# The second top-16 of a product-key router: 112 candidate sums instead of 256, and index lookups four heads at a time

## The chip, the cores and the metric

The kernel runs on one core of a Trainium2 chip. The metric is the device time of one execution in microseconds. The engines are named as in the profile: PE (TensorE matmul), PEld (its weight load), DVE (VectorE), ACT (ScalarE), POOL (GpSimd) and SP (SyncE, which issues most DMAs).

## The reference, cut to what matters

Two layers of a transformer over 256 latent and 256 context tokens. Each layer mixes tokens (attention, Fourier mixing, pooling) and then runs a feed-forward layer of 16,384 single-neuron experts, from which every token picks with product keys:

```
q = (h @ w_pq).reshape(B, L, 8, 2, 128)
s = einsum("blhpd,hpkd->blhpk", q, peer_keys)            # 8 heads, 2 halves, 128 keys
sv, si = top_k(s, 16)
cand = (sv[..., 0, :, None] + sv[..., 1, None, :]).reshape(B, L, 8, 256)
cidx = (si[..., 0, :, None] * 128 + si[..., 1, None, :]).reshape(B, L, 8, 256)
top_s, pos = top_k(cand, 16)
eidx = take_along_axis(cidx, pos, axis=-1)
gate = softmax(top_s, axis=-1)
```

So per token and head, 16 of 256 pair sums are selected, and the place of each selected sum says which first-half key and which second-half key it belongs to. Then `a = gelu(down[eidx] . h)`, and the output is the sum of `gate * a * up[eidx]`. Layer 0 does this for context and latent tokens, layer 1 for the latent ones only.

## The kernel before, in words

Tokens lie in blocks of 128, one token per partition. `scores` makes the key scores of two blocks and selects the best 16 of 128 of every half (`sv`, `si`). `topk` (L556) then does the second selection for one block on DVE: for each of 8 heads it adds the 16 x 16 pair sums (L562) and calls `top16` (L547 to L554), which finds eight maxima (L549), their places (L550), removes them (L551), and finds eight more (L553, L554). Behind the heads it copies the index table to bf16 (L568), makes the softmax gate (L571 to L575), splits the place `pos` into its two digits (L577, L578, L580), and looks the two key numbers up: for each half `w` and each two heads, a one-hot table of 32 x 16 is made by comparison with `iota16` (L586), multiplied by the index table (L589) and summed over its 16 columns (L591). `topk` is a generator; it yields twice a head and once a lookup, 24 times in all.

It is called six times. `early_routes` runs it twice, as the filler `extra` inside `front(0, 1, ...)`, the attention stage of the latent half of layer 0: `front` takes one step of the filler at six points of each of its 8 heads and drains the rest before the last projection. From the second of these calls come the expert numbers (L652) with which POOL then gathers rows of the expert tables (`rows`, L669). `routes` runs it twice in layer 0 and twice in layer 1: first a call alone, woven with `early` units (`fill`), then `gates` of the first block interleaved with a second call, woven with more units, and at last `gates` of the second block. How many units go with each step is fixed by the rates `R0` and `R1`.

A unit of `early` is `down` (L701 on): a 512 KB load of expert weights by SP in two parts, a split of each into a high and a low part on ACT (L83) and DVE (L84), 24 matmuls on PE (L93 to L95, 384 columns in layer 0, 256 in layer 1), a Gelu on ACT (L707) and a store. `gates` (L617 on) makes, for every four tokens, a comparison on DVE (L628, 1024 bf16 columns), a product (L632) and 12 matmuls of 128 columns (L638), and stores the expert gates; for a block of 128 tokens that is 32 times.

Working tiles come from tagged pools: `f1` (6 slots), `f2` (15 slots of 2 KB a partition) and `f8`. A tile that finds no free slot makes its first writer wait until a slot is released; a load waits on SP's queue, which runs in order.

Of the kernel before, what the change touches and what calls it, by code (L numbers as in the profile page):

```python
# [12 lines left out]
BF = mybir.dt.bfloat16  # L13
U32 = mybir.dt.uint32
I32 = mybir.dt.int32
AF = mybir.ActivationFunctionType
OP = mybir.AluOpType
AX = mybir.AxisListType
# [4 lines left out]
NH = 8  # L23
# [18 lines left out]
class Net:  # L42
# [101 lines left out]
    def setup2(self):  # L144
        nc, c, h = self.nc, self.c, self.h

        def ld(name, shape):
            t = c.tile(shape, F32, name=name)
            nc.sync.dma_start(t, h[name])
            return t  # L150

        self.g2 = ld("g2", [128, 2, 8])
        self.qg = ld("qg", [128, 2, 2])
        self.kg = ld("kg", [128, 2])
        self.bg = ld("bg", [128, 2, 24])
        self.hbg = c.tile([128, 2, 24], F32, name="hbg")
        nc.vector.tensor_scalar(self.hbg, self.bg, 0.5, None, op0=OP.mult)
        self.pscale = ld("pscale", [128, 2, 2])
        self.dup = ld("dup", [128, 128])
        self.tab = ld("tab", [128, TT])  # L160
        nc.sync.dma_start(self.xT[:, :, T:TT], h["xt"][:, :, T:TT])
        it = self.f1([128, 128])
        nc.sync.dma_start(it, h["iota"])
        self.iota = c.tile([128, 64, 2], BF, name="iotab")
        nc.vector.tensor_copy(self.iota.rearrange("p a b -> p (a b)"), it)
        self.iota16 = c.tile([128, 16], BF, name="iota16b")
        nc.vector.tensor_copy(self.iota16, it[:, 0:16])

    def mod_steps(self, l, *parts):
        nc, late = self.nc, None  # L170
# [385 lines left out]
    def topk(self, sv, si, out):  # L556
        nc, kp = self.nc, self.k
        ts = kp.tile([128, 8, 16], F32, name="tsc", bufs=1)
        pos = kp.tile([128, 128], U32, name="pos", bufs=1)
        for hd in range(NH):  # L560
            cd = self.f1([128, 16, 16])
            nc.vector.tensor_tensor(cd, sv[:, 2 * hd, :].unsqueeze(2).to_broadcast([128, 16, 16]),  # L562
                                    sv[:, 2 * hd + 1, :].unsqueeze(1).to_broadcast([128, 16, 16]), op=OP.add)
            scr = self.f1([128, 256])
            yield from self.top16(ts[:, hd, :], pos[:, hd * 16:(hd + 1) * 16], cd.rearrange("p a b -> p (a b)"), scr)
            yield
        sb = kp.tile([128, 16, 16], BF, name="sb", bufs=1)
        nc.vector.tensor_copy(sb, si)  # L568
        g = kp.tile([128, 8, 16], F32, name="gate", bufs=1)
        sm = kp.tile([128, 8, 2], F32, name="gsum", bufs=1)  # L570
        nc.vector.tensor_sub(g, ts, ts[:, :, 0:1].to_broadcast([128, 8, 16]))  # L571
        nc.scalar.activation(g, g, AF.Exp)
        nc.vector.reduce_sum(sm[:, :, 0], g, axis=AX.X)
        nc.vector.reciprocal(sm[:, :, 1], sm[:, :, 0])
        nc.vector.tensor_mul(g, g, sm[:, :, 1:2].to_broadcast([128, 8, 16]))  # L575
        pu = kp.tile([128, 2, 128], U32, name="pu", bufs=1)
        nc.vector.tensor_scalar(pu[:, 0, :], pos, 4, None, op0=OP.logical_shift_right)  # L577
        nc.vector.tensor_scalar(pu[:, 1, :], pos, 15, None, op0=OP.bitwise_and)  # L578
        pb = kp.tile([128, 2, 128], BF, name="pb", bufs=1)
        nc.vector.tensor_copy(pb, pu)  # L580
        ij = kp.tile([128, 2, 128], F32, name="ij", bufs=1)
        for w in range(2):
            for h2 in range(4):
                ks = slice(32 * h2, 32 * h2 + 32)
                oh = self.f1([128, 32, 16], BF)
                nc.vector.tensor_tensor(oh, self.iota16.unsqueeze(1).to_broadcast([128, 32, 16]),  # L586
                                        pb[:, w, ks].unsqueeze(2).to_broadcast([128, 32, 16]), op=OP.is_equal)
                o4 = oh.rearrange("p (h k) a -> p h k a", h=2)
                nc.vector.tensor_tensor(o4, o4, sb[:, 4 * h2 + w:4 * h2 + 4:2, :].unsqueeze(2).to_broadcast(  # L589
                    [128, 2, 16, 16]), op=OP.mult)  # L590
                nc.vector.reduce_sum(ij[:, w, ks], oh, axis=AX.X)  # L591
                yield
        out += [ij, g]

# [508 lines left out]
```

## Time and profile before

| what | value |
|---|---|
| median of three runs | 3143.14 us (3133.66 to 3145.1) |
| the profiled execution | 3146.14 us |
| its span in the profile | 3144.4 us |
| PE busy, share of the span | 2945.8 us, 94% |
| DVE busy | 2534.3 us, 81% |
| ACT busy | 1460.3 us, 46% |
| POOL busy | 323.9 us, 10% |

Busy time of an engine is time in which it ran an instruction; matmuls are pipelined and their ends are modelled, so PE shown as busy isn't PE at its peak. The profiled execution's time and its span differ by 1.7 us, which lie around the span.

### The profile page before, as it was taken

The page shows a single profiled execution, that of the slowest core. Times are in us where ns is not written, and L with a number is a line of the kernel's source. Part 1 is how long each engine was busy: PE and PEld are TensorE (multiplying, and loading weights), DVE is VectorE, ACT ScalarE, POOL GpSimd, SP SyncE. Part 2 cuts the span into 40 slices and gives each one's busy share as a digit, 9 for nine tenths or more (in the row PEclk, how much of TensorE's full clock was granted, in tenths as well). Part 3 has the DMA queues.
Part 4 walks back from the last instruction along what each step waited for, and adds up shares of the span by engine and source line. Part 5 has one row for each costly group of instructions (what it writes and reads, how often), then busy time and mean ns, then how long its engine had stood idle before and what let it go on. Part 6 is the DMA issues. An engine that isn't in the chain of part 4 may idle for free.

```text
span 3144.4 us, 55017 instructions
## 1 busy us (share of the span) xinstructions
PE 2945.8 (94%) x19215; PEld 2726.3 (87%) x19215; DVE 2534.3 (81%) x5831; ACT 1460.3 (46%) x2814; POOL 323.9 (10%) x260
## 2 busy tenths in 40 slices
PE   7999899798898999999999999999988889999998
PEld 5799878798888889999999998789877877799997
DVE  6677889798997889899999998566799966666666
ACT  5565444443444443344334434445544544555554
POOL 0000000111000121433333341000000000000000
PEclk8999999899999999999999999999998999999999
DMA  7574443675568878898988986454546788776664
GB/s 233 179 230 142 145 126 111 203 242 194 179 185 251 303 250 273 303 307 305 304 303 304 320 291 214 143 160 142 185 143 186 218 264 278 242 231 205 208 201 141
DMA packets 400719, 695.36 MB, mean 221 GB/s; under 512 B 36793, under 2 KB 148153, under 8 KB 396345
## 3 DMA queue, kind: packets, MB, share of 16 engines
q1 hardware_dynamic: 363576, 557.61, 54.8%
q0 software_dynamic: 36864, 134.23, 12.8%
q8 instruction: 151, 2.47, 0.3%
q14 instruction: 128, 1.04, 0.1%
HBM read 631.94 MB, written 59.77 MB: 220 GB/s over the span
## 4 chain that ended last, share of the span: by engine, by line
PE 65%; DVE 17%; DMA 11%; issue 5%; ACT 2%; SPq 0%; POOL 0%; DVEq 0%; ACTq 0%
PE mm L93 9%; PE mm L94 8%; PE mm L95 8%; PE acc L94 7%; PE acc L95 7%; PE acc L93 7%; DVE wl L84 4%; DMA ge<-E 2%; PE acc L818 2%; PE acc L819 2%; PE acc L817 2%; DVE a L632 2%; DMA raw<-in_up 2%; DMA raw<-in_wmod 1%; DVE f L628 1%
## 5 line engine op out<-in xcount | busy, mean ns | idle before, releaser
L83 ACT CAST wh<-raw 128x512 fp32r<-128x512 f32 x1604 | 981.4, 619 | 1006.4 <-PE acc L95 267.4
L84 DVE TENSOR_TENSOR wl<-raw,wh 128x512 fp32r<-128x512 f32 x1604 | 1075.7, 685 | 276.4 <-ACT wh L83 264.4
L93 PE MATMUL mm<-hH,wh 128*128 128x256 f32 (+1 forms) x2432 | 760.0, 313 | 43.1 <-ACT ge L707 38.9
L94 PE MATMUL mm<-hH,wl 128*128 128x256 f32 (+1 forms) x2432 | 757.1, 311 | 19.8 <-DVE wl L84 18.8
L95 PE MATMUL mm<-hL,wh 128*128 128x256 f32 (+1 forms) x2432 | 751.6, 309 | 0.0
L93 PEld LDWEIGHTS mm<-hH,wh 128*128 128x128 f32 x2432 | 468.3, 193 | 52.2 <-ACT ge L707 44.7
L94 PEld LDWEIGHTS mm<-hH,wl 128*128 128x128 f32 x2432 | 469.3, 193 | 28.6 <-DVE wl L84 25.6
L95 PEld LDWEIGHTS mm<-hL,wh 128*128 128x128 f32 x2432 | 468.7, 193 | 0.0
L94 PE MATMUL acc<-f,wl 128*128 128x384 f32 (+1 forms) x1216 | 402.1, 331 | 7.3 <-DVE wl L84 6.9
L95 PE MATMUL acc<-f,wh 128*128 128x384 f32 (+1 forms) x1216 | 400.4, 330 | 1.9 <-DVE f L731 1.9
L93 PE MATMUL acc<-f,wh 128*128 128x384 f32 (+1 forms) x1216 | 394.1, 330 | 8.0 <-ACT wh L83 2.9
L669 POOL DMA_INDIRECT gx<-in_down,eidx x128 | 184.6, 1442 | 1030.7 <-ACT f L250 573.7
L93 PEld LDWEIGHTS acc<-f,wh 128*128 128x128 f32 x1216 | 230.5, 190 | 14.2 <-issue 6.4
L94 PEld LDWEIGHTS acc<-f,wl 128*128 128x128 f32 x1216 | 232.3, 191 | 11.3 <-DVE wl L84 10.8
L95 PEld LDWEIGHTS acc<-f,wh 128*128 128x128 f32 x1216 | 232.1, 191 | 2.5 <-DVE f L731 2.2
L707 ACT ACTIVATE ge<-mm 128x384 f32<-128x384 f32 (+1 forms) x256 | 111.8, 437 | 241.6 <-PE mm L95 219.6
L728 DVE TENSOR_TENSOR ge<-ge,f 128x256 f32<-128x256 f32 (+1 forms) x384 | 132.6, 375 | 99.5 <-ACT ge L707 50.3
L93 PE MATMUL acc<-hH,wh 128*128 128x256 f32 x688 | 210.4, 306 | 1.3 <-ACT hH L280 1.2
L818 PE MATMUL acc<-wl,f 128*128 128x512 f32 x512 | 202.8, 396 | 7.5 <-DVE wl L84 7.2
L817 PE MATMUL acc<-wh,f 128*128 128x512 f32 x512 | 201.1, 393 | 1.0 <-ACT f L730 1.0
L819 PE MATMUL acc<-wh,f 128*128 128x512 f32 x512 | 200.8, 392 | 0.0
L94 PE MATMUL acc<-hH,wl 128*128 128x256 f32 x688 | 198.6, 289 | 0.1
(207 smaller groups left out, 4496.8 us busy)
## 6 DMA issues: line engine op xcount, KB each, us to landing
raw<-in_downT SPq DMA_DIRECT2D x512, 256.0 KB
raw<-in_up SPq DMA_DIRECT2D x512, 256.0 KB
raw<-in_wmod SPq DMA_DIRECT2D x192, 256.0 KB
raw<-in_winc SPq DMA_DIRECT2D x172, 256.0 KB
G<-f SPq DMA_DIRECT2D x40, 1024.0 KB
f<-G SPq DMA_DIRECT2D x32, 1024.0 KB
raw<-in_wpq SPq DMA_DIRECT2D x96, 256.0 KB
raw<-in_wo SPq DMA_DIRECT2D x48, 256.0 KB
```

The lines of the kernel that those rows point to most:

```text
L83: nc.scalar.copy(H, r)
L84: self.last = nc.vector.tensor_sub(L, r, H.bitcast(F32)).ins
L93: t.matmul(out, lhsT=wH, rhs=xH, start=first, stop=False)
L94: t.matmul(out, lhsT=wL, rhs=xH, start=False, stop=False)
L95: t.matmul(out, lhsT=wH, rhs=xL, start=False, stop=last)
L632: nc.vector.tensor_tensor(a, e[:, 0:4].unsqueeze(1).to_broadcast([128, 3, 4, 64, 2]), gT[:, t0 // 4].rearrange("p (x t) d -> p x t d", x=3 ...
L669: nc.gpsimd.indirect_dma_start(out=r, out_offset=None, in_=self.h["up"][0] if up else self.h["down0"], in_offset=bass.IndirectOffsetOnAxis ...
L707: nc.scalar.activation(a, p, AF.Gelu_apprx_tanh)
L728: nc.vector.tensor_mul(y, y, Gg[:, :, c, :])
L817: m(p[t][half], lhsT=aH[:, a], rhs=H[:, 0], start=(i == 0), stop=False)
L818: m(p[t][half], lhsT=aH[:, a], rhs=L[:, 0], start=False, stop=False)
L819: m(p[t][half], lhsT=aL[:, a], rhs=H[:, 0], start=False, stop=(i == 127))
```

## The change

The 16 values of each half are sorted. The new `topk` forms 112 of the 256 sums of a head: the first four values of one half with all 16 of the other (64 sums) and the other twelve with the first four (48 sums). They are made for four heads at once, in two instructions, in a tile of the `f2` pool. `pos` is decoded by four shifts and masks and three instructions that combine them. The lookups go over four heads at once, and the one-hot table has its 16 choices in the middle and the 16 places innermost, so the comparison's operands both have neighbouring elements; the index table is held with each entry twice side by side, and the sum runs over the middle. `topk` yields between the product and the sum of a lookup and behind the sum.

```diff
-        self.iota16 = c.tile([128, 16], BF, name="iota16b")
-        nc.vector.tensor_copy(self.iota16, it[:, 0:16])
+        self.iota16 = c.tile([128, 16, 16], BF, name="iota16b")
+        nc.vector.tensor_copy(self.iota16, it[:, 0:16].unsqueeze(2).to_broadcast([128, 16, 16]))
...
-        for hd in range(NH):
-            cd = self.f1([128, 16, 16])
-            nc.vector.tensor_tensor(cd, sv[:, 2 * hd, :].unsqueeze(2).to_broadcast([128, 16, 16]),
-                                    sv[:, 2 * hd + 1, :].unsqueeze(1).to_broadcast([128, 16, 16]), op=OP.add)
-            scr = self.f1([128, 256])
-            yield from self.top16(ts[:, hd, :], pos[:, hd * 16:(hd + 1) * 16], cd.rearrange("p a b -> p (a b)"), scr)
-            yield
-        sb = kp.tile([128, 16, 16], BF, name="sb", bufs=1)
-        nc.vector.tensor_copy(sb, si)
+        for h4 in range(2):
+            cd = self.f2([128, 4, 112])
+            ra, rb = sv[:, 8 * h4:8 * h4 + 8:2, :], sv[:, 8 * h4 + 1:8 * h4 + 8:2, :]
+            nc.vector.tensor_tensor(cd[:, :, 0:64].rearrange("p h (a b) -> p h a b", a=4),
+                                    ra[:, :, 0:4].unsqueeze(3).to_broadcast([128, 4, 4, 16]),
+                                    rb.unsqueeze(2).to_broadcast([128, 4, 4, 16]), op=OP.add)
+            nc.vector.tensor_tensor(cd[:, :, 64:112].rearrange("p h (a b) -> p h a b", a=12),
+                                    ra[:, :, 4:16].unsqueeze(3).to_broadcast([128, 4, 12, 4]),
+                                    rb[:, :, 0:4].unsqueeze(2).to_broadcast([128, 4, 12, 4]), op=OP.add)
+            for i in range(4):
+                hd = 4 * h4 + i
+                scr = self.f1([128, 112])
+                yield from self.top16(ts[:, hd, :], pos[:, hd * 16:(hd + 1) * 16], cd[:, i, :], scr)
+                yield
+
+        sb = kp.tile([128, 2, 128, 2], BF, name="sb", bufs=1)
+        for d in range(2):
+            nc.vector.tensor_copy(sb.rearrange("p w (h a) d -> p w h a d", h=8)[:, :, :, :, d],
+                                  si.rearrange("p (h w) a -> p w h a", w=2))
...
-        pu = kp.tile([128, 2, 128], U32, name="pu", bufs=1)
+        pu = self.f2([128, 4, 128], U32)
         nc.vector.tensor_scalar(pu[:, 0, :], pos, 4, None, op0=OP.logical_shift_right)
-        nc.vector.tensor_scalar(pu[:, 1, :], pos, 15, None, op0=OP.bitwise_and)
+        nc.vector.tensor_scalar(pu[:, 1, :], pos, 2, None, op0=OP.logical_shift_right)
+        nc.vector.tensor_scalar(pu[:, 2, :], pos, 15, None, op0=OP.bitwise_and)
+        nc.vector.tensor_scalar(pu[:, 3, :], pos, 3, None, op0=OP.bitwise_and)
         pb = kp.tile([128, 2, 128], BF, name="pb", bufs=1)
-        nc.vector.tensor_copy(pb, pu)
+        nc.vector.scalar_tensor_tensor(pb[:, 0, :], pu[:, 1, :], -12.0, pu[:, 0, :], op0=OP.add, op1=OP.max)
+        nc.vector.scalar_tensor_tensor(pb[:, 1, :], pu[:, 0, :], 4.0, pu[:, 2, :], op0=OP.is_lt, op1=OP.mult)
+        nc.vector.tensor_tensor(pb[:, 1, :], pb[:, 1, :], pu[:, 3, :], op=OP.max)
         ij = kp.tile([128, 2, 128], F32, name="ij", bufs=1)
         for w in range(2):
-            for h2 in range(4):
-                ks = slice(32 * h2, 32 * h2 + 32)
-                oh = self.f1([128, 32, 16], BF)
-                nc.vector.tensor_tensor(oh, self.iota16.unsqueeze(1).to_broadcast([128, 32, 16]),
-                                        pb[:, w, ks].unsqueeze(2).to_broadcast([128, 32, 16]), op=OP.is_equal)
-                o4 = oh.rearrange("p (h k) a -> p h k a", h=2)
-                nc.vector.tensor_tensor(o4, o4, sb[:, 4 * h2 + w:4 * h2 + 4:2, :].unsqueeze(2).to_broadcast(
-                    [128, 2, 16, 16]), op=OP.mult)
-                nc.vector.reduce_sum(ij[:, w, ks], oh, axis=AX.X)
+            for h4 in range(2):
+                ks = slice(64 * h4, 64 * h4 + 64)
+                oh = self.f2([128, 4, 16, 16], BF)
+                nc.vector.tensor_tensor(
+                    oh, self.iota16.unsqueeze(1).to_broadcast([128, 4, 16, 16]),
+                    pb[:, w, ks].rearrange("p (h k) -> p h k", h=4).unsqueeze(2).to_broadcast([128, 4, 16, 16]),
+                    op=OP.is_equal)
+                o4 = oh.rearrange("p h a (k d) -> p (h a) k d", d=2)
+                nc.vector.tensor_tensor(o4, o4, sb[:, w, ks, :].unsqueeze(2).to_broadcast([128, 64, 8, 2]), op=OP.mult)
+                yield
+                nc.vector.reduce_sum(ij[:, w, ks].rearrange("p (h k) -> p h k", h=4),
+                                     oh.rearrange("p h a k -> p h k a"), axis=AX.X)
                 yield
```

## Rows read from the trace of the kernel before

**Rows 1.** Busy us by stretch: PE, PEld, DVE, ACT, POOL, clock, DMA share, GB/s

```profile
416.00:551.00 135.00, 130.63 (x942) 115.68 (x942) 128.45 (x375) 59.48 (x125) 0.00 (x0) 1.00 0.34 107
551.00:573.00 22.00, 17.79 (x137) 16.47 (x136) 20.66 (x51) 9.49 (x19) 0.00 (x0) 1.00 0.36 113
788.00:837.00 49.00, 45.68 (x277) 44.97 (x275) 48.41 (x140) 20.64 (x36) 0.00 (x0) 0.97 0.64 200
837.00:937.00 100.00, 87.38 (x716) 81.81 (x714) 98.00 (x207) 43.08 (x76) 0.00 (x0) 0.95 0.58 174
...
2305.00:2351.00 46.00, 37.04 (x257) 34.89 (x258) 46.00 (x137) 17.07 (x33) 0.00 (x0) 0.85 0.46 150
2351.00:2464.00 113.00, 94.56 (x868) 89.91 (x867) 105.73 (x223) 51.47 (x97) 0.00 (x0) 0.89 0.63 194
```

**Rows 2.** Chain of waits, 546 to 590 us: start, duration, what

```profile
551.64 0.54 DVE ij L591
...
557.71 4.00 DMA raw<-in_wout
...
571.51 0.60 DVE ij L591
...
576.90 7.88 DMA gx<-in_down,eidx
```

**Rows 3.** PE groups by form, 788 to 837 us

```profile
L638 PE MATMUL acc<-a,f 128*128 128x128 bf16 x36 | 2.4, 220 | 0.0
```

**Rows 4.** Chain of waits, 788 to 840 us

```profile
788.03 1.36 PE acc L638 x24
...
797.14 0.17 PE mm L95
...
799.22 0.17 PE mm L95
```

**Rows 5.** PE in order of time, 2319 to 2341 us (twelve steps apart)

```profile
2323.07 0.28 PE L93 MATMUL mm<-hH,wh 128*128 128x256 f32 x1
...
2324.49 0.28 PE L93 MATMUL mm<-hH,wh 128*128 128x256 f32 x1
```

**Rows 6.** PE's waits, 2294 to 2351 us: total, times, longest

```profile
PE mm L94 <- DVE wl L84: 9.4, 3, 8.3
```

**Rows 7.** DVE in order of time, one head; eight instructions lie between

```profile
2317.54 0.42 DVE L562 TENSOR_TENSOR f<-sv 128x256 f32<-128x256 f32 x1
...
2319.72 0.68 DVE L84 TENSOR_TENSOR wl<-raw,wh 128x512 fp32r<-128x512 f32 x1
```

**Rows 8.** DVE groups by form, whole span: busy us, mean ns | idle before

```profile
L628 DVE TENSOR_TENSOR f<-iotab,ijT 128x1024 bf16<-128x1024 bf16 x160 | 105.2, 680 | 0.0
...
L553 DVE MAX8 sv<-scr 128x8 f32<-128x128 f32 x96 | 26.9, 280 | 0.1
...
L553 DVE MAX8 tsc<-f 128x8 f32<-128x256 f32 x48 | 20.0, 417 | 0.0
...
L615 DVE TENSOR_TENSOR gr<-gr,gT 128x128 f32<-128x128 f32 x5 | 1.4, 281 | 0.0
```

**Rows 9.** DVE in order of time, 2328 to 2352 us

```profile
2328.59 0.29 DVE L571 TENSOR_TENSOR gate<-tsc 128x128 f32<-128x128 f32 x1
2328.79 0.22 DVE L577 TENSOR_SCALAR pu<-pos 128x128 uint32<-128x128 uint32 x1
2328.93 0.23 DVE L578 TENSOR_SCALAR pu<-pos 128x128 uint32<-128x128 uint32 x1
...
2336.79 1.28 DVE L586 TENSOR_TENSOR f<-iota16b,pb 128x512 bf16<-128x512 bf16 x2
2337.99 0.76 DVE L589 TENSOR_TENSOR f<-f,sb 128x512 bf16<-128x512 bf16 x2
2338.66 1.27 DVE L591 TENSOR_REDUCE ij<-f 128x32 f32<-128x512 bf16 x2
2339.85 1.28 DVE L84 TENSOR_TENSOR wl<-raw,wh 128x512 fp32r<-128x512 f32 x2
```

## The prediction, made before the change was run

> **What bounds the kernel now.** I read the busy line of the page first: PE 94% and DVE 81% of the span, as the table above has it. An average over stages can't price this change, since `topk` runs only six times, so I found its six places by the starts of its L562 and asked for busy time in each [rows 1]. There are three kinds of place. (a) In the attention stage of the latent half, 416 to 573 us, two `topk` calls run as filler between the heads: PE is busy 130.6 of 135 us in the heads, so PE sets the pace and DVE (128.5 of 135) has almost no slack; in the eight merge steps behind them DVE is the tighter one (20.7 of 22 us) and the chain of waits runs through it, ends the lookups at 572 us with L591, and goes on through the first gathered row, 7.9 us [rows 2]. (b) In `routes` of layer 0, first call 788 to 837 us, second interleaved with the gates until 937 us. (c) In `routes` of layer 1, 2305 to 2351 and 2351 to 2464 us. In (b) and (c) DVE is busy 48.4 of 49, 98.0 of 100, 46.0 of 46 and 105.7 of 113 us [rows 1]. The reader is to see that four of the six calls stand where DVE has no free time, and that PE is close behind in one of these four.
>
> **What PE needs in the four stretches.** 788 to 837 holds 277 matmuls [rows 1], 36 of them of the gates [rows 3]; 24 of these take 1.36 us, and 12 of the 384-column ones take 2.08 us, 0.173 each [rows 4]. So 240 x 0.173 + 36 x 0.057 = 43.6 us: PE can't end this stretch before about 44 us. 837 to 937 holds 716, of which one `gates` call has 8 x 4 x 12 = 384: 332 x 0.173 + 384 x 0.057 = 79 us of 100. In layer 1 the early matmuls have 256 columns, 0.118 us each at full clock [rows 5]: 254 x 0.118 = 30 us of 46, and 484 x 0.118 + 22 = 79 us of 113. In the first of these PE has stood 8.3 us waiting for a weight split on DVE [rows 6] and the granted clock of the stretch is 0.85 [rows 1], part of it at the lower of the two levels; with that its need is nearer 36 to 39 us.
>
> **The change on DVE, per call.** Instructions on DVE overlap a little, so I price them by the step from start to start. One head of the old selection, nine instructions, takes 2319.72 - 2317.54 = 2.18 us [rows 7]. Max, index and replace at 128 columns take 280 ns where 256 take 417, 1.07 ns a column [rows 8]; that duration less the overlap of 0.08 us (0.68 long, 0.60 apart in the pairs of [rows 9]) is a step of 0.20. With the value loads at 0.065 (the nine steps less six of 0.33, by three) a head at 128 columns costs 5 x 0.20 + 0.2 = 1.2 us, at 112 columns 5 x 16 x 1.07 ns less, 1.1. The sums become two instructions per four heads, of 256 and 192 columns: 0.33 + 0.26, or 0.15 a head. New head 1.25, saved 0.93 x 8 = **7.4 us**.
>
> Lookups: a pair of old ones takes 2339.85 - 2336.79 = 3.06 us, so eight take 12.2: comparing 0.60, multiplying 0.34, reducing 0.60 each [rows 9]. The old comparison reads one operand with a repeated innermost element and goes at half the pace of the multiplication, which is as large. In the new layout both inputs of comparison and multiplication have neighbouring 2-byte elements innermost, as in L628, whose 1024 columns take 680 ns [rows 8], a step of 0.60. I take 0.60 for both. The reduction has 1024 elements at one per 1.07 ns: 0.60 + 512 x 1.07 ns = 1.14 us. Four lookups: 4 x 2.34 = 9.4, saved **2.9 us**. Bounds: the comparison might still run at the old pace, 1.14 instead of 0.60, which takes back 2.2 us a call. The reduction now steps by 16 elements, 32 bytes, between the elements it adds. No row of this trace shows such a step on DVE; the nearest reads every second 2-byte element (L615) and takes 281 ns at 128 columns, no more than the 280 of a maximum over 128 contiguous ones [rows 8]. I take no penalty, as the nearest row has none; the other end is a second cycle for every element, since a factor of two is all that separates two rates of one operation here (comparison and multiplication), and that is 4 x 1.1 = 4.4 us a call. A penalty can't be below nothing.
>
> [...]
>
> Small work: one more table copy, two more shifts, and three instructions of 128 columns in place of one copy. By the steps of 0.20 and 0.14 of these forms [rows 9]: 0.20 + 0.28 + 0.40 = **0.9 us** more. The `iota` table is widened once, under 1 us. Net 7.4 + 2.9 - 0.9 = **9.4 us** a call, 56 us of DVE in six. No DMA is added or moved; the yields stay 24 a call (16 + 8), so every filler unit falls into the same step as before. The Exp on ACT keeps its place, and so does the DVE gap behind it in 2351 to 2464.
>
> **What reaches the end.** (a) In the heads PE is the bound: only its 4.4 us of idle can go, and I count 3; at the merge steps three of the last lookups, from 551.64 to 571.51, lie on the chain (4.6 us), of which I count 3 as the index that starts the gathers comes earlier: 6. If DVE there were not late at all, this is 0; if all idle goes, 9. (b) 788 to 837: from 49 to PE's 44 and its half-clock time, **4**; 837 to 937: PE's 79 leaves room, **9.5**. (c) 2305 to 2351: PE's need stops it at about 39, **6.5**; 2351 to 2464: **9.5**. Sum 35.5 us. The profiled execution took 3146.14, 3.0 above the median of the runs; against its own time this is 3110.6, against the median 3107.6. I give **3108 us**.
>
> **Tile slots.** The pair sums of four heads, the shift results and the one-hot table move from the 6 small slots to the 15 of `f2`. In the heads I count ten live there (four `v`, the queries, two weights, one `K`, two transposes), so three more fit. I cost this at nothing; if they don't fit, a weight load on SP waits for its slot and everything behind it in that queue too.
>
> **Rivals.** 1: everything reaches the end (PE regains its full clock as it starves less, and follows): 3143 - 56 = 3087. For it: PE's idle and low clock in (b) and (c) are DVE's doing. Against: the 44 us of the first stretch and the heads. 2: the reduction takes two cycles an element: net 5.0 a call, 4 + 5 + 5 + 5 in (b) and (c) and 3 in (a), 22, so 3121. 3: the comparison doesn't speed up, so this part does not do what it says: net 7.2, 4 + 7.2 + 6.5 + 7.2 in (b) and (c) and 5 in (a), 30, so 3113. 4: in layer 1 the early units wait on Gelu, stores and loads in their queues instead, and in (a) nothing is won: the first call of layer 0 gives 4, each interleaved call half its saving, 5, and the first call of layer 1 nothing, 14, so 3129, no change that can be told. For it: PE's need at its low clock fills most of that last stretch; against it DVE at 46.0 of 46 and 98.0 of 100. 5: `f2` is short in the heads: six loads of `wq` and `wk` late by a landing of 4 us [rows 2], 24 us, against the 35: 3132. 6, the other side: the strided reduction costs four cycles. It decides from the point where four reductions lose 9.4 us, 2.35 each over 1.14, at 3.1 cycles an element; at four it is 3.3 x 4 = 13.1 us a call, a loss of 3.7, about 3 of it in each of the four tight calls and less in (a), some 15 us: 3158. Only that no row shows a stride of 32 bytes speaks for it.
>
> **How the numbers follow.** Chances: forecast 0.48, rival 1 0.14, 2 0.14, 3 0.05, 4 0.11, 5 0.04, 6 0.04. The measurement tells 0.5%, 15.7 us, from no change: below 3127.4 lie forecast and rivals 1 to 3, faster 0.81; rivals 4 and 5 make 0.15 the same; rival 6 slower 0.04. The range reaches from rival 1 with some clock regained (3084) to rival 4 (3129); the forecast's own is 3098 to 3118, from the bounds of (a) and of PE in the first stretches.
>
> **What would show it.** After: MAX8 of `tsc` at 112 columns near 263 ns; comparison and multiplication of 1024 near 0.68 us, the reduction near 1.22; DVE's busy time down by about 56 us; the stretch of the first call in layer 0 shorter by 4 to 5 us with PE full, the other three by 6 to 10 with DVE still full; the heads' stage nearly as long as before. A reduction of 2.3 us or more, a comparison of 1.2, a heads' stage longer than 135 us, or idle DVE in the four stretches would prove the steps above wrong.

## The result, and the profile after

The changed kernel takes 3117.88 us (median of 8 runs, 3108.96 to 3123.13) where the kernel before takes 3145.01 in the same series (8 runs): a ratio of 0.9908 [0.9893, 0.9923], some 29 us. The forecast was 3108, its own range 3098 to 3118. The profiled execution took 3108.96, nine below the median.

The groups by form of VectorE in the kernel after, over the whole span: busy us, mean ns of one, idle before. Line numbers are 19 higher than before behind `topk`.

```profile
L609 DVE TENSOR_REDUCE ij<-f 128x64 f32<-128x1024 bf16 x24 | 50.3, 2097 | 0.0
...
L607 DVE TENSOR_TENSOR f<-f,sb 128x1024 bf16<-128x1024 bf16 x24 | 16.3, 692 | 0.0
L602 DVE TENSOR_TENSOR f<-iota16b,pb 128x1024 bf16<-128x1024 bf16 x24 | 16.2, 688 | 0.0
L553 DVE MAX8 tsc<-f 128x8 f32<-128x112 f32 x48 | 12.8, 267 | 0.2
...
L565 DVE TENSOR_TENSOR f<-sv 128x256 f32<-128x256 f32 x12 | 5.0, 413 | 0.0
L568 DVE TENSOR_TENSOR f<-sv 128x192 f32<-128x192 f32 x12 | 4.2, 348 | 0.0
```

MAX8 at 112 columns (267 ns for the 417 of [rows 8]) and comparison and product (0.69 us each) are what the prediction took. The reduction is not: 2.10 us where 1.22 was expected. The order of time shows what it costs as a step from start to start (VectorE of the kernel after, first call of layer 1):

```profile
2306.00 0.71 DVE L602 TENSOR_TENSOR f<-iota16b,pb 128x1024 bf16<-128x1024 bf16 x1
...
2307.20 0.71 DVE L607 TENSOR_TENSOR f<-f,sb 128x1024 bf16<-128x1024 bf16 x1
...
2308.41 2.12 DVE L609 TENSOR_REDUCE ij<-f 128x64 f32<-128x1024 bf16 x1
2310.43 0.70 DVE L602 TENSOR_TENSOR f<-iota16b,pb 128x1024 bf16<-128x1024 bf16 x1
```

The reduction's step is 2310.43 - 2308.41 = 2.02 us, not 1.14: 0.88 more, four times a call, 3.5 us a call. Four lookups take 4 x (0.60 + 0.60 + 2.02) = 12.9 us where eight old ones took 12.2. Net a call: 9.4 - 3.5 = 5.9 us. The page agrees: VectorE's busy time falls from 2534.3 to 2501.6 us, 32.7, or 5.5 a call.

Where the time came from needs stretches that begin and end at the same work in both kernels. A is the start of the latent heads to the first gate matmul (two calls of `topk`), B from there to the last gate matmul of layer 0 (two calls), D layer 1 from the end of layer 0's experts to its last gate matmul (two calls). Stretches by engine of the kernel before, A, B and D: length, then busy us of PE, PEld, DVE, ACT, POOL, clock, DMA share, GB/s.

```profile
416.50:634.00 217.50, 196.84 (x1346) 175.75 (x1344) 193.97 (x515) 94.32 (x190) 12.38 (x11) 0.93 0.44 142
634.00:986.00 352.00, 319.59 (x2598) 305.01 (x2597) 330.98 (x817) 153.13 (x282) 25.48 (x16) 0.96 0.65 203
1966.00:2523.80 557.80, 507.71 (x4017) 465.64 (x4016) 449.19 (x1160) 272.13 (x531) 0.00 (x0) 0.95 0.54 169
```

The same three of the kernel after:

```profile
416.20:622.60 206.40, 190.03 (x1346) 171.89 (x1344) 182.67 (x491) 94.21 (x190) 9.83 (x10) 0.96 0.46 150
622.60:967.10 344.50, 315.39 (x2597) 301.43 (x2595) 319.96 (x796) 152.98 (x282) 28.01 (x17) 0.97 0.65 207
1941.70:2488.00 546.30, 500.31 (x4015) 460.25 (x4013) 436.67 (x1137) 271.66 (x531) 0.00 (x0) 0.97 0.55 173
```

A loses 11.1 us, B 7.5, D 11.5: 30.1 of the 37.3 by which the two profiled spans differ. The other 7 lie where no `topk` runs (layer 0's experts 980.0 and 974.6 us, and the rest); that experts' stretch takes 974 to 984 us in seven other profiled executions with nearly the same instructions in it and 992 in one more, so those 7 us are no gain of the change.

Windows of the kernel after that stand where [rows 1] has them: the heads of the attention stage, the merge steps up to the row index, and a window beside the first call of layer 0.

```profile
416.20:547.10 130.90, 127.93 (x920) 114.06 (x919) 118.24 (x357) 58.64 (x123) 0.00 (x0) 1.00 0.36 113
547.10:564.10 17.00, 15.68 (x129) 15.04 (x127) 16.80 (x36) 8.42 (x17) 0.00 (x0) 1.00 0.33 98
785.00:827.00 42.00, 42.00 (x261) 41.81 (x260) 39.28 (x106) 19.45 (x34) 0.00 (x0) 1.00 0.62 200
```

In the last of these rows TensorE is busy 42.00 of 42.00 us. But against the 49 us of [rows 1] it proves nothing, nor do the 91 us from 827 to 918 us against the 100 of [rows 1], since the windows don't hold the same work: by 787 us of the kernel after five of the eight heads of this call have had their first maxima, by 789 us of the kernel before one. So I cut B at a piece of work that both kernels have, the index transposes behind each call (the first cast of `ijT`). That gives the first call with what stands ahead of it, the second call with the gates of the first block, and the last gates. Before:

```profile
634.00:837.50 203.50, 184.45 (x1391) 179.30 (x1390) 184.19 (x542) 86.82 (x164) 25.48 (x16) 0.95 0.67 216
837.50:928.90 91.40, 78.78 (x657) 73.40 (x656) 90.42 (x188) 39.78 (x70) 0.00 (x0) 0.94 0.59 175
928.90:986.00 57.10, 56.37 (x554) 52.31 (x553) 56.36 (x90) 26.53 (x50) 0.00 (x0) 1.00 0.68 202
```

After:

```profile
622.60:819.50 196.90, 181.86 (x1390) 177.49 (x1389) 176.80 (x519) 86.87 (x164) 28.01 (x17) 0.97 0.69 223
819.50:913.80 94.30, 84.27 (x701) 79.03 (x700) 89.89 (x193) 42.22 (x75) 0.00 (x0) 0.96 0.62 194
913.80:967.10 53.30, 49.26 (x509) 44.91 (x508) 53.27 (x84) 23.89 (x45) 0.00 (x0) 1.00 0.57 170
```

The first part gives 6.6 us with the same matmuls in it. The second gives none and is 2.9 us longer: it holds 44 more matmuls of the early units, VectorE's busy time fell there by 0.5 us only, and VectorE idles 4.4 us where it idled 1.0. The last gates, which the change doesn't touch, are 3.8 us shorter with 45 fewer matmuls. D, cut in the same way up to the index transposes of its first and then of its second call, before:

```profile
1966.00:2351.00 385.00, 361.07 (x2555) 327.22 (x2554) 283.80 (x845) 190.09 (x377) 0.00 (x0) 0.96 0.50 156
2351.00:2464.30 113.30, 94.86 (x871) 90.21 (x870) 106.03 (x223) 51.77 (x98) 0.00 (x0) 0.89 0.63 195
```

After:

```profile
1941.70:2325.10 383.40, 361.67 (x2567) 329.30 (x2566) 278.64 (x832) 191.83 (x379) 0.00 (x0) 0.96 0.50 158
2325.10:2428.10 103.00, 86.78 (x855) 82.31 (x854) 99.32 (x215) 49.47 (x96) 0.00 (x0) 0.97 0.67 207
```

The first call of layer 1 gives 1.6 us here, the second 10.3.

### The profile page after: what moved, and what is told of

It is laid out like the page before. It is cut to its first block, busy times and chain, and to the rows that moved or that the text cites. A ratio compares the mean times of both kernels' runs of the same rounds, so it can differ in the third digit from the quotient of the medians.

```text
span 3107.1 us, 54952 instructions
## 1 busy us (share of the span) xinstructions
PE 2925.4 (94%) x19215; PEld 2717.1 (87%) x19215; DVE 2501.6 (81%) x5765; ACT 1459.4 (47%) x2814; POOL 327.9 (11%) x260
## 3 DMA queue, kind: packets, MB, share of 16 engines
q0 software_dynamic: 36864, 134.23, 12.9%
## 4 chain that ended last, share of the span: by engine, by line
PE 68%; DVE 17%; DMA 9%; issue 4%; ACT 1%; SPq 0%; DVEq 0%; ACTq 0%
PE mm L93 9%; PE mm L94 9%; PE mm L95 9%; PE acc L94 7%; PE acc L95 7%; PE acc L93 7%; DVE wl L84 3%; PE acc L837 3%; PE acc L836 3%; PE acc L838 3%; DVE a L651 2%; DMA raw<-in_up 2%; DVE f L647 2%; DMA ge<-E 1%; DVE xT L806 1%
## 5 line engine op out<-in xcount | busy, mean ns | idle before, releaser
L94 PE MATMUL acc<-hH,wl 128*128 128x256 f32 x688 | 198.4, 289 | 0.9 <-DVE wl L84 0.9
```

What stands on the lines that cost most here:

```text
L94: t.matmul(out, lhsT=wL, rhs=xH, start=False, stop=False)
```

## The experiments

**The reduction's step, undone.** Two layouts that read the 16 summands side by side, and one that doesn't use a reduction. First the plain one:

```diff
-                nc.vector.reduce_sum(ij[:, w, ks].rearrange("p (h k) -> p h k", h=4),
-                                     oh.rearrange("p h a k -> p h k a"), axis=AX.X)
+                nc.vector.reduce_max(ij[:, w, ks].rearrange("p (h k) -> p h k", h=4), oh, axis=AX.X)
```

> The changed kernel with one edit: the lookup's reduction reads its 16 elements next to each other (and takes their maximum), so it no longer gives the looked-up number; its count, sizes and place are the same. Theory A (the step of 32 bytes makes the reduction slow): it falls from 2.10 us to 1.22 us, DVE's busy time falls by 24 x 0.88 = 21 us against the changed kernel, and the time falls by 10 to 20 us to 3098 to 3108, a ratio to the kernel before of about 0.985 to 0.988. Theory B (the form is slow: 64 results of 16, three free dimensions, whatever the step): it stays near 2.1 us and the time stays at 0.991.

VectorE's groups by form in this run:

```profile
L609 DVE TENSOR_REDUCE ij<-f 128x64 f32<-128x1024 bf16 x24 | 29.0, 1207 | 0.0
```

1.21 us for 2.10, with the same 1024 elements, type and output. The edit also takes a maximum in place of a sum; e2, which keeps the sum, has the same 1.21 us, so the step of 32 bytes costs 0.89 us. The time did not follow: 3124.2 us, ratio 0.9919 [0.9894, 0.9944]. The profiled execution is the slowest of its six, 3129.1 us. In A, B and D the run takes 204.9, 345.7 and 541.9 us, 4.7 less than the kernel after; layer 0's experts take 991.7, 17 more. Here other rows are gathered, so that stretch isn't comparable; why it is longer I have not settled.

The second layout keeps the sums. The one-hot table has the 128 places outside and the 16 choices innermost, and the digits instead of the table entries stand twice:

```diff
-                oh = self.f2([128, 4, 16, 16], BF)
+                oh = self.f2([128, 64, 16], BF)
...
+                    oh.rearrange("p k (a d) -> p k a d", d=2),
+                    self.iota16.rearrange("p (a d) -> p a d", d=2).unsqueeze(1).to_broadcast([128, 64, 8, 2]),
+                    p2[:, w, ks, :].unsqueeze(2).to_broadcast([128, 64, 8, 2]), op=OP.is_equal)
...
+                nc.vector.reduce_sum(ij[:, w, ks], oh, axis=AX.X)
```

> The changed kernel with the lookups laid out the other way round: places outside, 16 choices innermost, the place digits held twice side by side instead of the table, and a contiguous reduction. Comparison and product keep neighbouring elements. Two copies that double the digits are added, one table copy is taken out. Theory A: comparison and product 0.69 us, reduction 1.22 us, DVE 18 to 21 us less than in the changed kernel, time 3100 to 3110, ratio 0.985 to 0.989. Theory B: reduction 2.1 us, ratio 0.991 or above.

```profile
L611 DVE TENSOR_REDUCE ij<-f 128x64 f32<-128x1024 bf16 x24 | 28.9, 1209 | 0.0
```

3106.94 us, ratio 0.9878 [0.9851, 0.9905]; VectorE 2482.8 us, 18.8 less than the kernel after. A and D are 3.1 and 4.7 us shorter than in the kernel after, B 1.1 longer. The interval of the ratio overlaps that of the change, so that e2 is faster than the change is shown by the stretches and not by the time.

The third keeps the layout of the change and adds halves, all contiguous:

```diff
-                nc.vector.reduce_sum(ij[:, w, ks].rearrange("p (h k) -> p h k", h=4),
-                                     oh.rearrange("p h a k -> p h k a"), axis=AX.X)
+                for n in (8, 4, 2):
+                    nc.vector.tensor_tensor(oh[:, :, 0:n, :], oh[:, :, 0:n, :], oh[:, :, n:2 * n, :], op=OP.add)
+                nc.vector.tensor_tensor(ij[:, w, ks].rearrange("p (h k) -> p h k", h=4), oh[:, :, 0, :], oh[:, :, 1, :],
+                                        op=OP.add)
```

> The changed kernel with the reduction replaced by four additions of halves (512, 256, 128 and 64 columns, bf16 but for the last result). Theory A: 0.42, 0.28, 0.22 and 0.21 us, all reading runs of neighbours; DVE's busy time falls by some 25 us and the time by 12 to 25 us, ratio 0.983 to 0.987. Against it: four dependent instructions in a row could each wait for the one before; if nothing stands between them they cost 1.1 us and more and the gain over one contiguous reduction is nothing, ratio 0.987.

Groups by form, VectorE, of this run:

```profile
L610 DVE TENSOR_TENSOR f<-f 128x512 bf16<-128x512 bf16 x24 | 9.9, 411 | 0.0
...
L610 DVE TENSOR_TENSOR f<-f 128x256 bf16<-128x256 bf16 x24 | 6.8, 281 | 0.0
L610 DVE TENSOR_TENSOR f<-f 128x128 bf16<-128x128 bf16 x24 | 5.2, 215 | 0.0
L611 DVE TENSOR_TENSOR ij<-f 128x64 f32<-128x64 bf16 x24 | 5.1, 213 | 0.0
```

Four adds, 1.12 us busy together, beat even the contiguous reduction. As steps from start to start they cost 0.34 + 0.20 + 0.14 + 0.14 = 0.82 us (from 2304.85, 2305.79, 2306.59 and 2307.33 us of this run), where the contiguous reduction of e2 costs 1.13. 3102.19 us, ratio 0.986 [0.9832, 0.9888]; VectorE 2470.9 us, 63.4 less than before. Stretches A, B and D of this run:

```profile
417.40:616.30 198.90, 188.98 (x1346) 171.31 (x1344) 175.00 (x516) 93.85 (x190) 12.27 (x11) 0.96 0.48 156
616.30:960.90 344.60, 314.22 (x2597) 299.79 (x2596) 310.19 (x819) 152.40 (x282) 25.37 (x16) 0.97 0.66 208
1943.90:2485.80 541.90, 501.30 (x4026) 462.28 (x4025) 428.59 (x1162) 271.77 (x531) 0.00 (x0) 0.96 0.56 174
```

Against the kernel after, VectorE is 7.7, 9.8 and 8.1 us less busy in A, B and D; A gives 7.5 of it and D 4.4. B gives nothing: 344.6 for 344.5.

**One half of the change alone.** The selection over 112 sums with the old lookups (L586 to L591 as before):

> The kernel before with the new selection and its decoding of places alone; lookups as before. By the rows of after, the selection saves 7.4 us a call and the decoding costs 0.7, 40 us of DVE in six calls. Theory A (DVE time in these places is worth 0.75 to 0.85 of itself, and the lookups of the change gain nothing because of the slow reduction): 28 to 34 us faster, ratio 0.989 to 0.991, the same as or better than the whole change. Theory B (the lookups carry part of the gain): less than 20 us, ratio above 0.9935.

3121.4 us, ratio 0.9894 [0.9877, 0.9911]; VectorE 2495.8 us, 6.4 less a call. The new lookups with the old selection over 256:

> The kernel before with the new lookups alone; the selection over 256 sums as before. Per lookup of four heads 0.60 + 0.60 + 2.02 us against two old ones of 3.06: 0.16 us more, four a call, and one more table copy, so about 0.9 us a call, 5 us of DVE in six, more than before. Theory A: no gain, ratio 0.998 to 1.003. Theory B: the lookups gain by their number alone, ratio below 0.996.

```profile
L595 DVE TENSOR_REDUCE ij<-f 128x64 f32<-128x1024 bf16 x24 | 50.0, 2085 | 0.0
```

3146.62 us against 3150.42, ratio 0.998 [0.9965, 0.9995]; VectorE 2538.5 us, 0.7 more a call. So with the stepped reduction the lookups' half wins no VectorE time, as the steps say (12.9 for 12.2), and selection alone does as well as the whole change. The few us that it does give lie in A (212.7 for 217.5), with VectorE as busy there as before; what shortens A I have not traced.

**One place alone.** A copy of the old `topk` serves one of the two places, the new one the other:

```diff
-        drain(weave(self.topk(*S[0], r0), fill, rates[0]))
+        drain(weave(self.topk_old(*S[0], r0), fill, rates[0]))
...
-        both = (x for pair in zip_longest(chunks(g0, 2), self.topk(*S[1], r1)) for x in pair)
+        both = (x for pair in zip_longest(chunks(g0, 2), self.topk_old(*S[1], r1)) for x in pair)
```

That leaves the change in the attention heads alone:

> The new code in the two calls inside the attention stage alone, the old one in the four calls of routes. The profile of after had the expert numbers 8.5 us earlier and the first gates 11 us earlier. Theory A (the merge steps and the first gathers wait for this call): 8 to 12 us faster, ratio 0.996 to 0.9975. Theory B, as the prediction had it (PE sets the pace there): 3 to 6 us, ratio 0.998 to 0.999.

3141.54 us, ratio 0.9967 [0.9953, 0.9982], some 10 us won (6 to 15). The other way round, the change in the four calls of the routes alone:

> The new code in the four calls of routes alone, the old one in the attention stage. With 5.9 us of DVE less a call: theory A 4 to 5 us in the first call of layer 0, where PE is full, and 4 to 6 in each of the others, 17 to 22 us faster, ratio 0.993 to 0.9945. Theory B (PE and the waits behind it take most of it back): under 10 us, ratio above 0.997.

3127.83 us, ratio 0.9912 [0.9888, 0.9935], some 28 us with a wide interval. Heads 10 and routes 28, against 29 for both at once: the heads' part agrees with A's 11.1, the routes' part has an interval of 20 to 35 us, just above B and D's 19.0, and in this run's own profile B is 7.7 and D 12.3 us shorter than before, 20.0. The two runs are a second pair of profiles for the parts above, e6 with the old routine there and e7 with the new: in B 203.3 and 198.4, 92.9 and 92.6, 57.7 and 53.3 us; in D, to the two index transposes, 389.8 and 382.2, 114.5 and 104.0 us. The matmuls moved in this pair too, 654 and 700 in the second part of B, 557 and 510 in the last.

**What holds B at 344 us.** Fewer early units beside the first selection call, more beside the second (and halving adds):

```diff
-SC0, SC1, R0, R1 = 0.5, 0.5, (0.36, 0.26, 0.22), (0.53, 0.4, 0.32)
+SC0, SC1, R0, R1 = 0.5, 0.5, (0.26, 0.32, 0.22), (0.53, 0.4, 0.32)
```

> Halving adds as in e3, and one constant more: in layer 0 the rates at which units of the experts are woven in go from (0.36, 0.26, 0.22) to (0.26, 0.32, 0.22), so that fewer units stand beside the first selection call of the routes and more beside the next two. Theory A (in the routes of layer 0 the time does not follow VectorE any more because TensorE is full beside the first call, 42.00 us of 42.00 in the kernel after): the stretch from the first gate matmul to the last one of layer 0 falls below the 344.6 us of e3 by up to 8 us, and the ratio to the kernel before comes to 0.983 to 0.985. Theory B (the order of the chunks and their eviction sets the floor, wherever the units stand): the stretch stays within 2 us of 344.6 and the ratio at 0.986. Theory C (VectorE still bounds the two later calls, as in the kernel before): the stretch gets longer by some 5 us, since more units' VectorE work stands there, and the ratio comes to 0.987 to 0.988.

3096.81 us, ratio 0.985 [0.9825, 0.9874], which can't be told from e3's 0.986. B itself is 345.2 us, the number of theory B; the reason that theory gives is not shown by it. The row of B in this run:

```profile
615.90:961.10 345.20, 317.72 (x2621) 303.53 (x2619) 311.75 (x821) 153.91 (x285) 30.09 (x16) 0.98 0.67 211
```

Its first part takes 189.4 us with 1342 matmuls where e3 has 199.6 with 1391, its second 102.5 with 773 where e3 has 91.7 with 701: the time moved along with the units and the sum stayed. Then less TensorE work, with VectorE's as it is:

```diff
-        self.mmk(p, W, lambda k: self.hH[:, k, t0:t0 + n], lambda k: self.hL[:, k, t0:t0 + n], 0, 8)
+        if l == 0:
+            for k in range(8):
+                (H, L), x = W[k // 4], self.hH[:, k, t0:t0 + n]
+                nc.tensor.matmul(p, lhsT=H[:, k % 4, :], rhs=x, start=(k == 0), stop=False)
+                nc.tensor.matmul(p, lhsT=L[:, k % 4, :], rhs=x, start=False, stop=(k == 7))
```

> Halving adds as in e3, with less TensorE work in layer 0: each block of the down projections there leaves out the product of the high half of the weights with the low half of the input, two matmuls in place of three, so that the values are only approximate; VectorE's and ScalarE's work is the same. Theory A (TensorE is the floor of 344.6 us in the routes of layer 0): the stretch falls by 15 us or more. Theory B (VectorE or the chain between chunks and their eviction is the floor): it falls by less than 5 us. The experts behind it get shorter by either theory.

B and its three parts (up to the index transposes of the first, then of the second call, then the last gates) in this run:

```profile
616.40:951.20 334.80, 269.25 (x2263) 248.60 (x2262) 309.00 (x818) 155.67 (x288) 27.18 (x16) 0.94 0.69 218
616.40:806.30 189.90, 159.03 (x1204) 150.84 (x1203) 169.98 (x528) 86.22 (x165) 27.18 (x16) 0.91 0.71 229
806.30:894.80 88.50, 67.45 (x602) 60.64 (x601) 85.24 (x207) 42.38 (x75) 0.00 (x0) 0.98 0.65 205
894.80:951.20 56.40, 42.77 (x461) 37.13 (x460) 53.78 (x85) 27.06 (x51) 0.00 (x0) 0.97 0.66 203
```

The same parts with all matmuls, in e3:

```profile
616.30:815.90 199.60, 183.72 (x1391) 179.03 (x1390) 171.69 (x531) 86.52 (x164) 25.37 (x16) 0.95 0.70 222
815.90:907.60 91.70, 81.23 (x701) 75.83 (x700) 85.21 (x205) 41.98 (x75) 0.00 (x0) 1.00 0.64 195
907.60:960.90 53.30, 49.27 (x509) 44.93 (x509) 53.29 (x84) 23.90 (x45) 0.00 (x0) 1.00 0.57 174
```

With 45.0 us less of TensorE's work B falls by 9.8, between the two theories' numbers. The first part gives 9.7, the second 3.2, and the last, with no `topk` in it and VectorE busy 53.29 of 53.3 us in e3, is 3.1 longer. And the same cut in the kernel before:

> The kernel before, with the same matmuls left out of layer 0's down projections as in e9. Theory A (in the kernel before VectorE, 331.0 us busy of 352.0, bounds the routes of layer 0, and TensorE only after the change): the stretch falls by less than 5 us from 352.0, a half or less of what e9 loses. Theory B (TensorE bounded it before too): it falls by as much as in e9, 15 us or more.

```profile
637.10:986.30 349.20, 279.02 (x2261) 258.03 (x2261) 330.30 (x816) 155.44 (x288) 27.18 (x16) 0.90 0.67 209
```

2.8 us less than the 352.0 of before, with 40.6 us less TensorE work: the number of the first theory. Set the runs beside each other by VectorE's busy time in B:

| run | VectorE busy in B, us | B, us |
|---|---|---|
| e5, lookups only | 333.5 | 351.1 |
| e6, old routine here | 331.5 | 353.9 |
| before | 331.0 | 352.0 |
| e7, new routine here | 320.1 | 344.3 |
| after | 320.0 | 344.5 |
| e4, selection only | 317.9 | 343.5 |
| e2, pair layout | 313.4 | 345.6 |
| e1, contiguous maximum | 313.3 | 345.7 |
| e8, halving adds and rates | 311.8 | 345.2 |
| e3, halving adds | 310.2 | 344.6 |
| e10, before, fewer matmuls | 330.3 | 349.2 |
| e9, halving adds, fewer matmuls | 309.0 | 334.8 |

From 331 to 320 the stretch follows VectorE, and below 320 it stays at 343.5 to 345.7 whatever VectorE saves, until matmuls are left out. What VectorE saved and B did not give is idle time of VectorE, 21.0 us in B before, 24.5 after and 34.4 in e3, and the growth lies in one of its waits, the one for the high part of a weight split, which ScalarE makes (total, times, longest; B before, after and in e3):

```profile
DVE wl L84 <- ACT wh L83: 17.2, 9, 6.2
DVE wl L84 <- ACT wh L83: 21.8, 14, 5.4
DVE wl L84 <- ACT wh L83: 30.2, 19, 6.3
```

ScalarE's splits in turn wait in B of e3 34.5 us for loads of expert weights and 27.8 for matmuls of earlier units; in e9 the matmuls hold them 10.4 us, and the loads 55.0. So the floor is in the chain of the early units, from load to split to matmul. Which of its links sets 344 us no run here separates.

## Why the prediction came out as it did

The measured 3117.88 us lies inside the forecast's own range by 0.1 us, 10 above 3108, and nearer to rival 2 (3121) and rival 3 (3113) than to 3108. The mechanism held in outline: VectorE's time, saved where VectorE has next to no slack, reaches the end (23.8 us less in A and D gave 22.6). The sizes of the terms did not hold, and that their sum stayed in the range is in part luck: (a) gave 5.1 us more than its term, (b) 6.0 less and (c) 4.5 less.

**The step that failed first: "I take no penalty, as the nearest row has none."** The nearest row was no model for this one: it reads every second 2-byte element, and the new reduction has a step of 32 bytes. The penalty is 0.89 us of 2.10 by duration, shown by e1 and e2 (1.21 us each), which change the order of the elements and leave their number, their type and the output as they were. So the lookups save nothing on VectorE (e5: 0.7 us a call lost, where 2.9 were to be won), and the net is 5.9 us a call, not 9.4. This is rival 2's mechanism at a little less than its size: it asked for 5.0 a call and gave 3121; I gave it 0.14.

**(c) fell short with that, and its halves came out otherwise.** Forecast 6.5 + 9.5, measured 11.5 in D, near the two calls' 2 x 5.9. When the sums were made contiguous D fell further, to 541.6 and 541.9, near the forecast 16. But the first call gave 1.6 us (7.6 between e6 and e7) where 6.5 were forecast, and the second 10.3 (10.5), where VectorE saved 6.7. The clock of the second call's part rose from 0.89 to 0.97, and that is not the reason: e6, with the old routine, has 0.96 there and takes 114.5 us. What else lengthened the old call I have not separated. Whether "2305 to 2351: PE's need stops it at about 39" was right can't be read, since in the kernel after the first call's sums begin at 2280.9 us and its index transposes come at 2325.1, so no window holds the same work.

**(b) was mis-sized for another reason.** Forecast 4 + 9.5, and with the true reduction that would be 4 + 5.9 = 9.9; B gave 7.5 (9.6 between e6 and e7), and 6.4 and 7.4 with the sums contiguous. The step that failed is "837 to 937: PE's 79 leaves room, 9.5". The first call's part gave 6.6, more than its 4, so TensorE's need did not stop it there; the second call's part and the gates behind it gave 0.9 together (4.7 between e6 and e7). The prediction also took it that "every filler unit falls into the same step as before", because the yields stay 24. They do stay, and yet 44 more matmuls of the early units stand ahead of the second call's index transposes and 45 fewer behind them, with 26 weight splits on VectorE in that part for 23. Why they moved is open. Idle VectorE in the four stretches was the prediction's own sign of being wrong, and it appeared: 4.4 us in the second call's part. Below 320 us of VectorE's busy time B has a floor near 344.5, of which at least 9.8 us hang on TensorE's work (e9). The rates are not it (e8), and 53.3 us of B are VectorE in gates, which the change does not touch.

**(a) was under-sized.** Forecast 3 in the heads and 3 at the merge steps; measured 1.6 (132.5 to 130.9) and 6.6 (23.6 to 17.0, from the last head to the row index), and another 2.9 from the row index to the first gate matmul (61.4 to 58.5; 60.8 in e6, so this last piece scatters by as much). The chain of waits of the kernel after still runs through the lookups here, and from the last of them to the gather:

```profile
558.30 2.02 DVE ij L609
...
564.19 0.20 DVE eidx L671
...
565.34 5.54 DMA gx<-in_down,eidx
```

At the merge steps VectorE was the bound, busy 21.55 of 23.6 us before and 16.80 of 17.0 after, with 51 instructions and with 36. The 3 us were counted for the three last lookups, and they are not where the gain came from: nine instructions of lookups, 4.6 us as steps, became two stepped reductions of 4.0. What else went is four of ten weight splits, 2.4 us as steps, which now run outside this stretch, some smaller pieces, and 1.9 of its 2.1 us of idle time. That this came to more than the count is luck. The first gathered row is used at 570.9, before at 580.2 (the gather of 7.88 us in [rows 2] is that of the third row).

**Rivals.** Rival 1 (all of it reaches the end) is nearly what A and D did, of a smaller saving: A and D together give 22.6 us for 23.8 us less VectorE; B stands against it. Rival 2 has the mechanism that was measured, 0.88 us more a reduction where it took 1.1, and its 3121 is the nearest of all the forecasts to 3117.88. Rival 3 is out: the comparison takes 688 ns. Rival 4 fails at (a), where it gave nothing and 11.1 us came; of its other terms, nothing for the first call of layer 1 is near the 1.6 of this pair. Rival 5 is out: it asked for 24 us of late loads, and the heads' stage is 1.6 us shorter. Rival 6 is out: the step is 0.88 us over the forecast's 1.14, and it decides from 2.35 over. With the measured reduction the forecast's own sum would have been 6 + 4 + 3 x 5.9 = 27.7 us, against some 29 by the ratio: what (a) gave above its term, 5.1, is more than the 2.4 and 0.3 that (b) and (c) would then have held back, with 3115 to 3116 as the result.

## What to carry to other kernels

Before you lay a table out for the instructions that write it, price the one that reads it: here the layout that made the comparison twice as fast a column (a step of 0.60 us for 1024 columns, where it was 0.60 for 512) put 32 bytes between the summands (2.10 us a reduction for 1.21), and took it all back (12.9 us for four lookups, 12.2 for the eight old ones). Sum such a table by halving adds over contiguous halves, or turn the layout so that the summands are innermost (ratios 0.986 and 0.9878 for 0.9908, the second's interval touching that of the change). And where filler is woven in, cut the trace of both kernels at the same piece of work before you compare: windows by the clock showed 9 us of gain for the second call of layer 0 (100 to 91), where the part cut by work is 2.9 us longer. An engine that is given time back may only wait for the next link: here VectorE's saved time came back in B as waits for weight splits on ScalarE (17.2 us before, 21.8 after, 30.2 in e3).

## What the hardware showed that I had not expected

Four contiguous adds of 512, 256, 128 and 64 columns of 2-byte values (411, 281, 215 and 213 ns) are shorter than one contiguous reduction of the 1024 (1207 ns), which is a single instruction: 1.12 us together against 1.21, and against 2.10 with the step of 32 bytes.

With 1024 matmuls left out the kernel was slower, against what was expected of the experts. The kernel before took 3176.1 us without them (one run) against a median of 3148.6, and e9 3120.3 (one run) against 3102.2 of e3. In e9 B is shorter, but layer 0's experts behind it take 1010.2 us where e3 has 983.0, with 75.6 us less TensorE work in them. Rows of that stretch, e9:

```profile
951.20:1961.40 1010.20, 872.72 (x4622) 819.73 (x4622) 880.40 (x1778) 383.83 (x718) 325.70 (x229) 0.96 0.83 279
```

and e3:

```profile
960.90:1943.90 983.00, 948.36 (x5327) 925.90 (x5327) 877.52 (x1779) 385.46 (x724) 343.72 (x229) 0.98 0.85 289
```

TensorE's idle time there grows from 34.6 to 137.5 us, 39.6 of it behind weight splits on VectorE (1.3 in e3) and 36.3 behind those on ScalarE (1.8), and the granted clock falls from 0.98 to 0.96, a mean over the stretch (in the kernel before it reads 1.00 from 2321 to 2353 us, and 0.50 from 2309 to 2317 us, behind 6 us without a matmul). The splits come later because they wait for their loads, as ScalarE's waits in that stretch show, e3 and then e9:

```profile
ACT wh L83 <- DMA raw<-in_up: 50.7, 36, 4.7
ACT wh L83 <- DMA raw<-in_up: 255.7, 95, 6.5
```

Its waits for loads of `in_downT` grow from 16.8 to 108.9 us, those for the matmuls of the sums fall from 144.8 to 63.4, and the kernel before shows the same without its matmuls (48.6 to 261.6 us for `in_up`). Why the loads then set a pace slower than that of TensorE with all its matmuls is open.
